# Row blocks of 113 and 15 rows per partition instead of 112 and 16 in a streaming ReLU row sum

## The chip, the cores and the metric

One core of a Trainium2 chip runs the kernel. The metric is the device time of one execution in microseconds (us), median over several runs.

## The reference

```python
def setup_inputs():
    return {"x": np.random.randn(32, 512, 1024).astype(np.float32)}

def reference(x):
    relu_x = np.maximum(x, 0)
    return np.sum(relu_x, axis=-1).astype(np.float32)
```

67.11 MB come in, 16,384 sums of 4 bytes go out.

## The kernel before

The 16,384 rows are two blocks. In the first, partition p holds 112 rows that follow each other in memory, in the second 16. So the input is read at a pitch of 448 KiB and 64 KiB from partition to partition, and the results of one partition are 448 and 64 bytes that follow each other in the output.

```python
REGIONS = [112, 16]
CHUNKS = [(0, 0), (0, 16), ..., (0, 96)]     # 7 loads of 16 rows per partition
TAIL = [8, 4, 2, 1]                          # then pieces of the second block
LAST = [512, 512]                            # and its last row in two halves

    xv = [xr[P * s : P * (s + n), :].rearrange("(p j) d -> p j d", p=P) for s, n in zip(start, REGIONS)]
    ov = [of[P * s : P * (s + n)].rearrange("(p j) -> p j", p=P) for s, n in zip(start, REGIONS)]
    # ... all loads are issued by SyncE into three buffers, then:
    sp.wait_ge(s_fact, 1)                    # last rows of chunk 6 are summed
    sp.wait_ge(s_fdve, 1)
    for g in range(len(REGIONS) - 1):        # the first store: 128 pieces of 448 bytes
        sp.dma_start(out=ov[g][:, :], in_=res[:, start[g] : start[g] + REGIONS[g]]).then_inc(s_store, 16)
    # ... ScalarE and VectorE share the rows; at the end ScalarE sums the first half of the
    # last row, VectorE adds the second half to it:
    on_act(buf[:, tb, BIG - 1, 0 : LAST[0]], last[:, LAST[1] : LAST[1] + 1]).then_inc(s_tact, 1)
    dve.wait_ge(s_tact, 1)
    dve.wait_ge(s_in[-1], 16)
    on_dve(last[:, :], res[:, J - 1 : J]).then_inc(s_tdve, 1)
    sp.wait_ge(s_tdve, 1)                    # the last store: 128 pieces of 64 bytes
    sp.dma_start(out=ov[-1][:, :], in_=res[:, start[-1] : J]).then_inc(s_out, 16)
    sp.wait_ge(s_store, 16 * (len(REGIONS) - 1))
    sp.wait_ge(s_out, 16)
```

## Time and profile before

| | before |
|---|---|
| time, median of the first 3 runs | 161.53 us |
| span of the profiled run | 159.9 us |
| one chunk of 8 MiB after the other | 19.35 us |
| last store, issue to landing | 1.4 us |

The prediction below shows the main lines. In the list of DMA issues a line has the size and the time from the issue to the landing, that is until the store has been confirmed:

```profile
out_dram<-res SPq DMA_DIRECT2D x1, 56.0 KB, 10.6
out_dram<-res SPq DMA_DIRECT2D x1, 8.0 KB, 1.4
```

The first store takes 10.6 us: it is issued at 147.20, but its packets run from 156.70 to 157.28, at the end of those of the loads, the last of which is over at 157.10. The second one takes 1.4 us with nothing else in flight. All 1.4 us of it lie on the path, as the last of SyncE's own waits shows (total, number, longest, in us):

```profile
SPq L165 <- DMA out_dram<-res: 1.1, 1, 1.1
```

The wait of 1.1 us at the end is the last store, after its issue of 0.34 us. The time can so be read as four terms that add up: the time until ScalarE can start on the first chunk (21.82), the stretch of loads until it starts on the first half of the last row (to 156.95), the sums and hand-overs until the last store is issued (to 158.45), and the store until the end (to 159.9).

### The profile page before, as it was taken

Reading aid. Unit: us, or ns where it says so; the run is one execution under the profiler, and the core shown is the slowest. Engines: PE = TensorE matmul, PEld = TensorE weight load, DVE = VectorE, ACT = ScalarE, POOL = GpSimd, SP = SyncE. Lnnn points to the kernel's source line nnn. Section 1 sums busy time; section 2 is a strip of 40 time slices with the busy share of each in tenths; the row PEclk is TensorE's granted clock in tenths of the full one; section 3 lists DMA queues with packets and bytes.
Section 4 is the critical chain, followed back from the end, with each engine's and each line's share of the span. In section 5 each row is a group of like instructions: output and inputs, shape, how many; then the busy total and the mean of one; then the engine's idle time right before and its main releaser. Section 6 shows DMA issues by size and latency. Waiting matters only on the chain.

```text
span 159.9 us, 145 instructions
## 1 busy us (share of the span) xinstructions
DVE 122.0 (76%) x56; ACT 101.0 (63%) x55; POOL 0.2 (0%) x4
## 2 busy tenths in 40 slices
DVE  0000006989889897998969989699899999598995
ACT  3000059990799708996099941999339980596972
POOL 0000000000000000000000000000000000000000
DMA  7996996996996997997989979969969969899993
GB/s 262 525 525 262 525 525 262 525 525 262 525 508 279 525 459 328 525 443 344 525 361 426 525 311 475 525 262 525 525 262 525 525 262 525 385 402 393 420 409 105
DMA packets 2160, 67.18 MB, mean 420 GB/s; under 512 B 496, under 2 KB 496, under 8 KB 880
## 3 DMA queue, kind: packets, MB, share of 16 engines
q1 hardware_dynamic: 2160, 67.18, 97.9%
HBM read 67.11 MB, written 0.07 MB: 420 GB/s over the span
## 4 chain that ended last, share of the span: by engine, by line
DMA 69%; ACT 18%; DVE 10%; SPq 1%; issue 0%
DMA buf<-in_x_dram 69%; ACT buf L128 18%; DVE res L130 10%; SPq L88 1%; ACT buf L108 0%; DVE last L111 0%
## 5 line engine op out<-in xcount | busy, mean ns | idle before, releaser
L130 DVE TENSOR_REDUCE res<-buf 128x4 f32<-128x4096 f32 (+3 forms) x18 | 100.4, 5604 | 33.5 <-ACT buf L128 33.5
L128 ACT ACTIVATE buf<-buf 128x4096 f32<-128x4096 f32 (+3 forms) x18 | 80.8, 4553 | 46.3 <-DMA buf<-in_x_dram 46.3
L108 ACT ACTIVATE buf<-buf 128x1024 f32<-128x1024 f32 (+1 forms) x18 | 18.4, 1021 | 9.7 <-DMA buf<-in_x_dram 9.7
L111 DVE TENSOR_SCALAR_CACHE_REDUCE buf<-buf 128x1024 f32<-128x1024 f32 x18 | 21.0, 1216 | 2.7 <-DMA buf<-in_x_dram 2.5
L108 ACT ACTIVATION_READ_ACCUMULATOR buf<-buf 128x1 f32 x18 | 3.4, 187 | 0.0
L128 ACT ACT_TABLE_LOAD x1 | 1.3, 1283 | 0.8 <-PEq L179 0.8
L111 DVE DVE_READ_ACCUMULATOR buf<-buf 128x1 f32 x18 | 1.5, 82 | 0.0
L111 DVE TENSOR_SCALAR_CACHE_REDUCE last<-last 128x513 f32<-128x513 f32 x1 | 0.7, 690 | 0.2 <-ACT buf L108 0.2
L179 POOL MEMSET const-uint8-127<- 128x1 uint8 x1 | 0.1, 103 | 0.0
L179 POOL MEMSET const-bfloat16-1.0<- 128x1 bf16 x1 | 0.1, 102 | 0.0
L179 POOL MEMSET const-float32-0.0<- 128x1 f32 x1 | 0.1, 99 | 0.2 <-issue 0.2
L179 POOL MEMSET const-float32-1.0<- 128x1 f32 x1 | 0.1, 99 | 0.0
L111 DVE DVE_READ_ACCUMULATOR last<-last 128x1 f32 x1 | 0.1, 82 | 0.0
## 6 DMA issues: line engine op xcount, KB each, us to landing
buf<-in_x_dram SPq DMA_DIRECT2D x1, 4096.0 KB, 26.7
buf<-in_x_dram SPq DMA_DIRECT2D x1, 2048.0 KB, 31.2
buf<-in_x_dram SPq DMA_DIRECT2D x1, 1024.0 KB, 33.2
buf<-in_x_dram SPq DMA_DIRECT2D x1, 512.0 KB, 34.0
buf<-in_x_dram SPq DMA_DIRECT2D x1, 256.0 KB, 34.2
last<-in_x_dram SPq DMA_DIRECT2D x1, 256.0 KB, 34.4
buf<-in_x_dram SPq DMA_DIRECT2D x7, 36.3
out_dram<-res SPq DMA_DIRECT2D x1, 56.0 KB, 10.6
```

What stands on the lines that cost most here:

```text
L88: sp.dma_start(out=buf[:, tb, r : r + n, :], in_=xv[-1][:, r : r + n, :]).then_inc(s_in[NBIG + i], 16)
L108: return act.activation(t, t, AF.Relu, accum_out=acc)
L111: return dve.tensor_scalar(out=t, in0=t, scalar1=0.0, scalar2=None, op0=ALU.max, op1=ALU.add, accum_out=acc)
L128: act.activation(t, t, AF.Relu).then_inc(s_act, 1)
L130: dve.tensor_reduce(out=res[:, c * BIG + r : c * BIG + r + n], in_=t, axis=X, op=ALU.add).then_inc(s_dve, 1)
L179: nc = _bacc.Bacc("TRN2", target_bir_lowering=False, num_devices=1)
```

## The change

The row blocks become 113 and 15 rows. Row 112 of the first block is loaded as the last whole piece of the tail. So both pitches of the input change (452 and 60 KiB), the last store has 15 columns instead of 16, and the first one, now of 113 columns, can only go out when row 112 is summed. The intent is a smaller store at the very end, and pitches that are no multiples of 64 KiB; that either saves time no run here had shown.

```diff
-REGIONS = [112, 16]
+REGIONS = [113, 15]
-TAIL = [8, 4, 2, 1]
+TAIL = [(1, 0, 8), (1, 8, 4), (1, 12, 2), (0, 112, 1)]     # region, first row, rows
@@ loads of the tail
-    for i, n in enumerate(TAIL):
-        sp.dma_start(out=buf[:, tb, r : r + n, :], in_=xv[-1][:, r : r + n, :]).then_inc(
+    for i, (g, j, n) in enumerate(TAIL):
+        sp.dma_start(out=buf[:, tb, r : r + n, :], in_=xv[g][:, j : j + n, :]).then_inc(
@@ the first store
     sp.wait_ge(s_fact, 1)
     sp.wait_ge(s_fdve, 1)
+    sp.wait_ge(s_rdve, 1)
@@ sums of the tail
-        for i in range(r, r + n):
-            f = on_act if (i - r) % 2 else on_dve
-            f(buf[:, tb, i, :], res[:, j0 + i : j0 + i + 1])
+        for i in range(n):
+            f = on_act if i % 2 else on_dve
+            ins = f(buf[:, tb, r + i, :], res[:, j + i : j + i + 1])
+    ins.then_inc(s_rdve, 1)
```

More of the change, by code (lines that the diff above doesn't have):

```diff
@@ L36, in bass_relu_sum_kernel @@
     NBIG = len(CHUNKS)
-    assert BIG * NBIG + sum(TAIL) + 1 == J == sum(REGIONS) and sum(LAST) == D
+    assert BIG * NBIG + sum(n for _, _, n in TAIL) + 1 == J == sum(REGIONS) and sum(LAST) == D
     xr = x.rearrange("b s d -> (b s) d")
@@ L57, in bass_relu_sum_kernel @@
     s_fdve = nc.alloc_semaphore("s_fdve")
+    s_rdve = nc.alloc_semaphore("s_rdve")
     s_tact = nc.alloc_semaphore("s_tact")
@@ L86, in bass_relu_sum_kernel @@
     tail = []
-    for i, n in enumerate(TAIL):
-        sp.dma_start(out=buf[:, tb, r : r + n, :], in_=xv[-1][:, r : r + n, :]).then_inc(
+    for i, (g, j, n) in enumerate(TAIL):
+        sp.dma_start(out=buf[:, tb, r : r + n, :], in_=xv[g][:, j : j + n, :]).then_inc(
             s_in[NBIG + i], 16
         )
-        tail.append((r, n, s_in[NBIG + i]))
+        tail.append((r, n, s_in[NBIG + i], start[g] + j))
         r += n
-    sp.dma_start(out=buf[:, tb, r, 0 : LAST[0]], in_=xv[-1][:, BIG - 1, 0 : LAST[0]]).then_inc(
+    sp.dma_start(out=buf[:, tb, r, 0 : LAST[0]], in_=xv[-1][:, REGIONS[-1] - 1, 0 : LAST[0]]).then_inc(
         s_in[-2], 16
     )
-    sp.dma_start(out=last[:, 0 : LAST[1]], in_=xv[-1][:, BIG - 1, LAST[0] : D]).then_inc(
+    sp.dma_start(out=last[:, 0 : LAST[1]], in_=xv[-1][:, REGIONS[-1] - 1, LAST[0] : D]).then_inc(
         s_in[-1], 16
@@ L136, in bass_relu_sum_kernel @@
                 on_act(*row(c, i))
-    j0 = NBIG * BIG
     for c in range(NTWO, NBIG):
@@ L146, in bass_relu_sum_kernel @@
                 ins.then_inc(s_fact if i % 2 else s_fdve, 1)
-    for r, n, s in tail:
+    for r, n, s, j in tail:
         if n > 1:
```

## The prediction

> **What bounds the kernel now.** I read four views in this order: the summary page, the chain of work that ended last in order of time, the timeline of the engines, and the DMA view of the last five microseconds. The page first:
>
> ```profile
> span 159.9 us, 145 instructions
> DMA packets 2160, 67.18 MB, mean 420 GB/s; under 512 B 496, under 2 KB 496, under 8 KB 880
> DMA 69%; ACT 18%; DVE 10%; SPq 1%; issue 0%
> ```
>
> The input of 67.11 MB has to come in once. The mean of 420 GB/s is over the whole span, head and tail included. The rate in the steady part comes from the timeline, from the starts of ScalarE's work on two successive 8 MiB chunks:
>
> ```profile
> 21.82 14.04 ACT L128 ACTIVATE buf<-buf 128x4096 f32<-128x4096 f32 x3 [19.75 <-DMA buf<-in_x_dram]
> ...
> 41.13 14.04 ACT L128 ACTIVATE buf<-buf 128x4096 f32<-128x4096 f32 x3 [5.27 <-DMA buf<-in_x_dram]
> ...
> 60.48 3.62 ACT L128 ACTIVATE buf<-buf 128x4096 f32<-128x4096 f32 x1 [5.32 <-DMA buf<-in_x_dram]
> ...
> 99.19 14.04 ACT L128 ACTIVATE buf<-buf 128x4096 f32<-128x4096 f32 x3 [5.30 <-DMA buf<-in_x_dram]
> ```
>
> Each chunk lands 19.35 us after the one before it (60.48 - 41.13, and twice that from 60.48 to 99.19), whatever the compute engines do, and ScalarE waits over 5 us for each. 8,388,608 bytes in 19.35 us is 433.5 GB/s. So the loads are the bound from the first byte on, and the compute parts that the chain shows lie beside loads. What remains beyond the loads is the end:
>
> ```profile
> 122.75 34.18 DMA buf<-in_x_dram
> 156.93 0.02 issue
> 156.95 0.73 ACT buf L108 x2
> 157.68 0.05 issue
> 157.73 0.69 DVE last L111 x2
> ```
>
> After the first half of the last row has landed at 156.93, ScalarE sums it (0.73 us), VectorE sums the other half with that result (0.69 us), and the last store goes out. The timeline of the same stretch shows VectorE's last whole row and the two stores:
>
> ```profile
> 147.20 0.35 SPq L102 DMA_DIRECT2D out_dram<-res  x1
> ...
> 156.28 1.22 DVE L111 TENSOR_SCALAR_CACHE_REDUCE buf<-buf 128x1024 f32<-128x1024 f32 x1
> ...
> 157.43 0.08 DVE L111 DVE_READ_ACCUMULATOR buf<-buf 128x1 f32 x1
> ...
> 158.45 0.34 SPq L163 DMA_DIRECT2D out_dram<-res  x1
> ```
>
> The DMA view from 155 to 160 us, 40 slices of 0.125 us, shows when the DMA engines are busy:
>
> ```profile
> DMA  9997999999999998320000000000000000330000
> ```
>
> Loads and the first store fill it up to slice 17 (157.2 us). Then there is nothing for about 2 us, and the two digits in slices 34 and 35 (159.25 to 159.5) are the last store. The first store, though issued at 147.20, landed 10.6 us later, at 157.8; the last one took 1.4 us.
>
> [...] the first store's 448-byte packets start at 156.70, 9.5 us after the issue[...].
>
> **The change part by part.**
>
> 1. The amount and order of loading. Seven chunks of 16 rows, then pieces of 8, 4, 2, 1 rows and two halves, as before: 67.11 MB, the same number of transfers of the same sizes from the same engine. Order of instructions and waits on VectorE and ScalarE is the same line by line; only the first store has one wait more. Change: 0.
>
> 2. The addresses. Row blocks start every 452 KiB instead of 448, and in the second region every 60 KiB instead of 64. Rows stay multiples of 4 KiB. Could the tail gain from the new pitch? The packet records give the mean time of one packet on its engine, by size: 65,536 B 2418 ns (median), 32,768 B 1213, 16,384 B 615, 8,192 B 312, 4,096 B 159, 2,048 B 86. From the first two, 32,768 B cost 1205 ns, which is 27.2 GB/s for one engine and 435 for 16; what is left over is 8 to 11 ns a packet at every size. From 137.90 (the last chunk has landed) to 156.93, 15.5 rows of 524,288 B come in, 8.126 MB, which at 433.5 GB/s is 18.75 us; it took 19.03. The difference of 0.28 us is what the extra packets cost: per engine 5 x 8 = 40 packets instead of 7.75 for the same bytes in 64 KiB packets, some 32 x 9 ns = 0.29. Nothing is left over for the pitch of 64 KiB to explain. Change: 0.
>
> 3. The first store moves. Before it waited for the last rows of chunk 6 (147.0); now for row 112, which is the last whole row of the tail. VectorE is done with it at 157.43 + 0.08 = 157.51. From VectorE's end to the issue of the last store before is 158.45 - 158.42 = 0.03 us, so the first store is issued at about 157.54 and SyncE is free again at 157.89, 0.56 us before it has to issue the last store. The last store's first packet came at 159.29, 0.84 us after its issue; so the first store's packets start near 158.38. Each engine has 8 of them at 25 ns, 0.2 us, and the engines are spread over some 0.2 us, as the last store's were (159.29 to 159.50): they end near 158.8. The last store's packets begin at 159.29, on empty queues again. With the 0.35 us from last packet to landing that the last store shows, the first store lands near 159.15, 0.7 us before the last. Estimates all, from these rows. On the path: 0. Loads are not helped either: the first store stood behind them.
>
> 4. The last store writes 128 x 60 bytes instead of 128 x 64. Packets of 64 B take 8 to 11 ns; 4 bytes less is worth nothing. Pieces of 60 bytes no longer start on multiples of 64, so neighbouring partitions write into the same 64 bytes. I allow 0.05 us for this.
>
> 5. A semaphore increment at row 112's sum on VectorE: it is attached to an instruction that is there anyway. VectorE was done at 157.51 and waited for ScalarE until 157.68, so even 0.1 us would be hidden.
>
> Sum: +0.05 us on a span of 159.9; the time is 1.63 us over the span before (161.53), so 161.58, which I round to 161.6.
>
> **The rivals.** First: the pitch matters, and the tail gets faster.[...] Against it: the packet times of point 2. At most the 0.28 us would be won: 161.3. Second: the new pitch does harm. Transfers of 64 KiB no longer start on 64 KiB; if each were cut once more, 56 more packets per engine at 8 ns would cost 0.45 us: 162.0.[...] Third: the two stores collide, and the last waits behind the first, or the first lands last. The margin is about 0.5 us by point 3; if the first store were to begin 0.5 us later than I think, the last would be put off by the 0.2 us of its packets, or its landing would set the end: up to 0.3 us, 161.8. Fourth: the unaligned 60-byte writes land in 1.8 instead of 1.4 us: 162.0.
>
> **Range and chances.** All but one of these lie between 161.3 and 162.0. Times of before lie within 0.05 us on one chip; another chip or day may move by some 0.1 us more. I give 161.3 to 162.1 for 8 in 10. Faster by 2% would need 3.2 us, and no more than 0.3 is there to be had: 0.01. Slower by 2% needs a loading rate 2% lower, which only the new pitch could bring: 0.02. Within 2%: 0.97.
>
> **What would show it right or wrong.** Right: chunks still land 19.35 us apart; the first half of the last row lands within 0.1 us of 156.93; the last five microseconds of the DMA view show a second island of digits near 158.4 to 158.8 that was joined to the loads before; the first store's time to landing falls from 10.6 to about 1.6 us; the last store's stays at 1.4 to 1.5. Wrong: chunks further apart than 19.5 us or nearer than 19.3 (the pitch matters after all), a last store that takes over 1.7 us, or a wait of SyncE at the end that is put down to the first store.

## The result, and the profile after

The changed kernel takes 161.99 us (median of 6 runs, 161.94 to 162.39), the kernel before 161.56 (6 runs, 161.49 to 161.76). The ratio is 1.0029, with a 95% interval of 1.0016 to 1.0042. A ratio here is the mean time of one kernel's fast runs over that of the other's of the same rounds, so it is not quite the ratio of the medians. The change costs 0.3%, far within 2%, but it is clear of the noise.

The profiled run was the longest of the six (162.39). Its page:

```profile
span 160.7 us, 145 instructions
DMA packets 2160, 67.18 MB, mean 418 GB/s; under 512 B 496, under 2 KB 496, under 8 KB 880
```

As many packets and bytes as before. The timeline has the start of the chunks:

```profile
22.20 14.04 ACT L130 ACTIVATE buf<-buf 128x4096 f32<-128x4096 f32 x3 [20.14 <-DMA buf<-in_x_dram]
...
41.52 14.04 ACT L130 ACTIVATE buf<-buf 128x4096 f32<-128x4096 f32 x3 [5.27 <-DMA buf<-in_x_dram]
...
60.88 3.62 ACT L130 ACTIVATE buf<-buf 128x4096 f32<-128x4096 f32 x1 [5.32 <-DMA buf<-in_x_dram]
```

The first chunk is there 0.38 us later than before (22.20 against 21.82). From then on a chunk takes 19.36 us (60.88 - 41.52), as it did. The end of the chain of waits:

```profile
123.18 34.14 DMA buf<-in_x_dram
157.31 0.02 issue
157.34 0.73 ACT buf L110 x2
158.07 0.02 issue
158.09 0.70 DVE last L113 x2
```

157.34 - 22.20 is 135.14 us; before it was 156.95 - 21.82 = 135.13. The whole stretch of loads, tail with its new pitch included, is unchanged to 0.01 us. The two stores in SyncE's timeline:

```profile
158.00 0.35 SPq L104 DMA_DIRECT2D out_dram<-res  x1
158.82 0.34 SPq L165 DMA_DIRECT2D out_dram<-res  x1
```

The last one is issued 1.48 us after ScalarE's start at 157.34 (before: 1.50). The DMA engines from 155 to 160 us, in slices of 0.125 us as in the prediction:

```profile
DMA  8999999999999962100000000000001870000430
```

The predicted second island is there: the first store's packets, in slices 30 to 32 (158.75 to 159.125; by the packet records they end at 159.19). They are done before the last store's packets begin (slices 37 and 38). The list of issues and SyncE's wait at the end:

```profile
out_dram<-res SPq DMA_DIRECT2D x1, 56.5 KB, 2.0
out_dram<-res SPq DMA_DIRECT2D x1, 7.5 KB, 1.8
```

```profile
SPq L167 <- DMA out_dram<-res: 1.5, 1, 1.5
```

The last store takes 1.8 instead of 1.4 us, although it moves less. The span has grown by 0.8 us, of which 0.38 came before the first chunk and 0.43 (160.71 - 158.82 = 1.89, before 159.91 - 158.45 = 1.46) after the last store's issue. This run is 0.4 us longer than the changed kernel's median, so not all of the 0.8 us is the change. That was the question for the experiments.

### The profile page after: what moved, and what is told of

Its sections match the earlier page's. It is cut to its first block, busy times and chain, and to the rows that moved or that the text cites. A ratio compares the mean times of both kernels' runs of the same rounds, so it can differ in the third digit from the quotient of the medians.

```text
span 160.7 us, 145 instructions
## 1 busy us (share of the span) xinstructions
DVE 122.0 (76%) x56; ACT 101.0 (63%) x55; POOL 0.2 (0%) x4
## 2 busy tenths in 40 slices
DMA packets 2160, 67.18 MB, mean 418 GB/s; under 512 B 496, under 2 KB 496, under 8 KB 880
## 3 DMA queue, kind: packets, MB, share of 16 engines
q1 hardware_dynamic: 2160, 67.18, 97.4%
## 4 chain that ended last, share of the span: by engine, by line
DMA 69%; ACT 18%; DVE 10%; SPq 1%; issue 0%
DMA buf<-in_x_dram 69%; ACT buf L130 17%; DVE res L132 9%; SPq L89 1%; ACT buf L110 0%; DVE last L113 0%
```

## The experiments

They went out in three calls, each on one chip, each run with five rounds against the kernel before on the same chip. The numbers are in this table, which is worked out from the profiles: start of ScalarE on the first chunk; from there to its start on the last row's first half; from there to the issue of the last store; from there to the end of the span. Row pitch is that of the loads in rows, pieces are those of the first and the last store in bytes.

| run | pitch | pieces | first chunk | loads | sums | last store | ratio (95% interval) |
|---|---|---|---|---|---|---|---|
| before | 112 | 448, 64 | 21.82 | 135.13 | 1.50 | 1.46 | |
| changed | 113 | 452, 60 | 22.20 | 135.14 | 1.48 | 1.89 | 1.0029 (1.0016 to 1.0042) |
| e1_late_store | 112 | 448 late, 64 | 21.89 | 135.14 | 1.48 | 1.50 | 1.0002 (0.9989 to 1.0014) |
| e2_store_shape | 112 | 452, 60 | 21.95 | 135.14 | 1.50 | 2.09 | 1.0038 (1.0024 to 1.0052) |
| e3_load_pitch | 113 | 448, 64 | 22.01 | 135.12 | 1.51 | 1.46 | 1.0009 (0.9996 to 1.0021) |
| e4_row112_first | 113 | 452, 60 | 21.99 | 135.20 | 1.60 | 1.82 | 1.0047 (1.0034 to 1.0059) |
| f1_source_shift | 112 | 448, 64 | 21.76 | 135.15 | 1.52 | 1.45 | 1.0004 (0.9991 to 1.0016) |
| f2_own_line | 112 | 448, 60 of 64 | 21.95 | 135.14 | 1.51 | 1.59 | 1.0006 (0.9992 to 1.0020) |
| f3_pieces_32 | 120 | 480, 32 | 21.96 | 135.18 | 1.48 | 1.46 | 1.0016 (1.0003 to 1.0028) |
| f4_pieces_16 | 124 | 496, 16 | 22.06 | 135.21 | 1.47 | 1.47 | 1.0029 (1.0016 to 1.0042) |
| g_last_60 | 112 | 448, 60 | 21.83 | 135.13 | 1.50 | 1.47 | 1.0005 (0.9994 to 1.0017) |
| g_last_48 | 112 | 448, 48 | 21.94 | 135.12 | 1.48 | 1.67 | 1.0016 (1.0004 to 1.0028) |
| g_last_4 | 112 | 448, 4 | 21.75 | 135.13 | 1.50 | 6.98 | 1.0340 (1.0311 to 1.0370) |
| g_last_64_shift | 112 | 448, 64 shifted | 21.88 | 135.15 | 1.49 | 1.47 | 0.9991 (0.9978 to 1.0004) |

A profile is one run, while the ratio is of five or six, so the terms of a row and its ratio need not agree to 0.1 us. The first call ran on chip 2, the second on chip 14, the third on chip 11. In the diffs below, new semaphores and lines that only repeat a change are cut.

### First call: pitch, lateness, or the shape of the stores

The theory (W) was that stores in unaligned pieces take longer to be confirmed. Rivals were that two stores close together hurt (S), and that the new pitch of the loads costs at the start (P).

**e1_late_store** moves the first store alone:

```diff
     sp.wait_ge(s_fdve, 1)
+    sp.wait_ge(s_rdve, 1)
@@ after the loop over the tail
-            f(buf[:, tb, i, :], res[:, j0 + i : j0 + i + 1])
+            ins = f(buf[:, tb, i, :], res[:, j0 + i : j0 + i + 1])
+    ins.then_inc(s_rdve, 1)
```

> The kernel before with one thing moved: its first store (112 columns, aligned) waits for the last whole row of the tail, as in the changed kernel. Theory W (the 60- and 452-byte pieces, which are not aligned to 64 bytes, take about 0.4 us longer to be confirmed): 161.6 us, the last store lands 1.4 us after its issue. Rival S (two stores 0.8 us apart get in each other's way, or the last store's completion waits for the writes of the first): 162.0 us, the last store lands after about 1.8 us. Rival P (the new pitch of the loads costs 0.4 us): 161.6 us.

Measured: 161.53 us against 161.47. The result is right. The list of issues of this run:

```profile
out_dram<-res SPq DMA_DIRECT2D x1, 56.0 KB, 1.6
out_dram<-res SPq DMA_DIRECT2D x1, 8.0 KB, 1.5
```

The stores are as close together as in the changed kernel (issued at 157.69 and 158.51), and it costs nothing that the timing shows (1.0002, interval 0.9989 to 1.0014). S falls as a matter of lateness alone. There is a second reading: the same late first store takes 1.6 us in pieces of 448 bytes and 2.0 us in pieces of 452.

**e2_store_shape** keeps the loads of before and stores 113 and 15 columns, the first store early:

```diff
-    ov = [... for s, n in zip(start, REGIONS)]
+    OUTS = [113, 15]
+    ostart = [0, 113]
+    ov = [... for s, n in zip(ostart, OUTS)]
@@ and res[:, ostart...] in both stores; the first waits for the first row of the tail
```

> The loads of before (pitch of 112 and 16 rows), but the results are stored as 113 and 15 columns, 452 and 60 bytes a piece, the first store early (its wait is met by the first row of the tail, near 149 us). The result is wrong on purpose (rows end up at other places of the output). Theory W: 162.0 us, the last store lands about 1.8 us after its issue. Rival S: 161.6 us and 1.4 us. Rival P: 161.6 us.

Measured: 162.12 us against 161.47; the result is wrong. The list of issues:

```profile
out_dram<-res SPq DMA_DIRECT2D x1, 56.5 KB, 8.9
out_dram<-res SPq DMA_DIRECT2D x1, 7.5 KB, 2.0
```

The first store was issued at 149.07 and had landed at 158.0, before the last was issued at 158.59. Nothing of the loads has changed, and the last store takes 2.0 us. The shape of the stores is enough to cost what the change costs, as W expects.

**e3_load_pitch** is the other half: the loads of the changed kernel, the stores of before.

```diff
+    OUTS = [112, 16]
+    ostart = [0, 112]
-    ov = [... for s, n in zip(start, REGIONS)]
+    ov = [... for s, n in zip(ostart, OUTS)]
-    sp.wait_ge(s_rdve, 1)
```

> The loads of the changed kernel (pitch of 113 and 15 rows), but the results are stored as 112 and 16 columns, early and aligned, as before. The result is wrong on purpose. Theory W: 161.6 us, the last store lands after 1.4 us. Rival S: 161.6 us. Rival P: 162.0 us, with the first chunk landing some 0.4 us later than the 21.8 us of before, as it did in the profile of the changed kernel (22.2).

Measured: 161.61 us against 161.47, wrong. The last store takes 1.4 us again:

```profile
out_dram<-res SPq DMA_DIRECT2D x1, 8.0 KB, 1.4
```

The first chunk is there at 22.01, and the ratio of 1.0009 has an interval that includes 1. So P is not the main part. It may be a small one, though: in the table, the first chunk comes at 21.75 to 21.95 in all nine profiles with a pitch of 112 rows (mean 21.86), and at 21.96 to 22.20 in all five with another pitch (mean 22.04). The gap of 0.18 us is about what e3 shows in its ratio (0.0009 x 161.5 = 0.15 us). It is suggested by the profiles, and not settled by the timing: the latest of the nine and the earliest of the five lie only 0.01 us apart, and the runs were not all on one chip.

**e4_row112_first** leaves the changed kernel as it is but loads row 112 first, so that its first store goes out early:

```diff
-TAIL = [(1, 0, 8), (1, 8, 4), (1, 12, 2), (0, 112, 1)]
+TAIL = [(0, 112, 1), (1, 0, 7), (1, 7, 4), (1, 11, 2), (1, 13, 1)]
-    ins.then_inc(s_rdve, 1)
+            if r == 0:
+                ins.then_inc(s_rdve, 1)
```

> The changed kernel with row 112 loaded first of the tail (pieces of 1, 7, 4, 2, 1 rows and two halves), so that its first store goes out some 10 us earlier, behind the loads as before; the last store keeps its 60-byte pieces. One transfer more, worth under 0.1 us. The result is right. Theory W: 162.0 us, the last store lands after 1.8 us. Rival S: 161.6 us and 1.4 us. Rival P: 162.0 us and 1.4 us.

Measured: 162.29 us against 161.47, right. The list of issues, and the end of the chain of waits:

```profile
out_dram<-res SPq DMA_DIRECT2D x1, 56.5 KB, 9.6
out_dram<-res SPq DMA_DIRECT2D x1, 7.5 KB, 1.8
```

```profile
157.98 0.02 DVEq L161
158.00 0.07 issue
158.07 0.69 DVE last L113 x2
```

Taking the first store out of the end does not bring the 1.8 us back to 1.4. W holds here too. Its ratio is 0.3 us above the changed kernel's; the profile shows 0.06 us of that in the loads (one transfer more) and 0.12 in the sums. VectorE's last piece of work starts 0.07 us after ScalarE's sum, because the second half of the last row was confirmed at 157.95: three of its 16 confirmations came 0.25 us after the other 13. The first store's packets run at that time (156.76 to 157.54; before the change 156.70 to 157.28).

### Second call: what about those pieces

**f1_source_shift** moves the last 16 results one column on in SBUF, so that the last store reads from the same address in the row as the changed kernel's, and writes as before:

```diff
-    res = nc.alloc_sbuf_tensor("res", [P, J], fp32)
+    res = nc.alloc_sbuf_tensor("res", [P, J + 1], fp32)
-    sp.dma_start(out=ov[-1][:, :], in_=res[:, start[-1] : J]).then_inc(s_out, 16)
+    sp.dma_start(out=ov[-1][:, :], in_=res[:, start[-1] + 1 : J + 1]).then_inc(s_out, 16)
```

> The kernel before, its output pieces unchanged (64 bytes, aligned to 64), but the last 16 results lie one column further on in SBUF, so that the last store reads from an address that is 452 bytes into the row, as in the changed kernel. The result is right. Theory D (what costs 0.4 us is where the pieces lie in the output): same as before, the last store lands 1.4 us after its issue. Rival R (it is the unaligned address that is read): 1.8 us, and 0.4 us more of time.

Measured: 161.53 us against 161.56, right, with 1.4 us to landing. The address that is read made no difference here. R falls.

**f2_own_line** writes 60 bytes, but each piece within its own 64:

```diff
-    sp.dma_start(out=ov[-1][:, :], in_=res[:, start[-1] : J]).then_inc(s_out, 16)
+    sp.dma_start(out=ov[-1][:, 1:], in_=res[:, start[-1] + 1 : J]).then_inc(s_out, 16)
```

> The kernel before, but the last store leaves out the first of its 16 columns: 60 bytes a piece, each within 64 bytes of its own, since the pieces still start every 64 bytes (at 4). The result is wrong on purpose, column 112 is not written. Theory L (two partitions that write into the same 64 bytes are what costs): 1.4 us to landing, as before. Rival F (a piece that does not fill its 64 bytes costs, shared or not): 1.8 us, 0.4 us more of time.

Measured: 161.60 us against 161.56, wrong. 1.5 us to landing. Pieces that don't fill their 64 bytes cost 0.1 us here (interval -0.1 to 0.3), less than the 0.4 us that F expects, so F falls as stated.

**f3_pieces_32** and **f4_pieces_16** are right versions of the kernel with other blocks:

```diff
-REGIONS = [113, 15]
-TAIL = [(1, 0, 8), (1, 8, 4), (1, 12, 2), (0, 112, 1)]
+REGIONS = [120, 8]                                          # f3
+TAIL = [(0, 112, 8), (1, 0, 4), (1, 4, 2), (1, 6, 1)]
+REGIONS = [124, 4]                                          # f4
+TAIL = [(0, 112, 8), (0, 120, 4), (1, 0, 2), (1, 2, 1)]
```

(Cut: in both, the first store waits for the sums of the last two rows of the first block, one on VectorE and one on ScalarE.)

> Row blocks of 120 and 8 rows: pieces of 480 bytes, and at the end of 32 bytes, which start on multiples of 32; two partitions share each 64 bytes. The first store waits for row 119, near 152 us, and lies behind the loads. The result is right. If pieces have to be whole units of 64 bytes: about 1.8 us to landing and 0.4 us over before. If units of 32 bytes are enough: 1.4 us and no difference.

> Row blocks of 124 and 4 rows: pieces of 496 bytes, and at the end of 16 bytes, four partitions to each 64 bytes, two to each 32. The first store waits for row 123, near 155 us. The result is right. With units of 64 or of 32 bytes: 1.8 us or more to landing, 0.4 us or more over before, more than the pieces of 32 bytes if the number of partitions that share a unit counts. If it were only that pieces straddle a boundary, these would not: 1.4 us and no difference.

Measured: 161.74 and 161.98 us against 161.56. In both profiles the last store takes 1.4 us, as if sharing 64 bytes among two or four partitions cost nothing. But f4's profiled run was the fastest of its five (161.71; the others 161.94 to 162.22), and where the others lost 0.2 to 0.5 us more can't be read from it. The 0.2 and 0.3 us that the two profiles do show lie before the first chunk (0.14 and 0.24) and in the loads (0.05 and 0.08). These two runs are inconclusive on the store.

### Third call: the last store alone

The last store of before is replaced and nothing else. Three theories on what in its pieces costs were to be told apart: two DMA engines write into the same 64 bytes (E; which engine writes which partition no trace here shows, so what E forecasts for each run rests on an assumption), pieces straddle multiples of 64 (B), pieces start elsewhere than on multiples of 16 (M).

```diff
-    sp.dma_start(out=ov[-1][:, :], in_=res[:, start[-1] : J]).then_inc(s_out, 16)
+    n = 15                                # g_last_60; 12: g_last_48; 1: g_last_4
+    tight = of[P * start[-1] : P * (start[-1] + n)].rearrange("(p j) -> p j", p=P)
+    sp.dma_start(out=tight, in_=res[:, J - n : J]).then_inc(s_out, 16)
```

```diff
+    sp.wait_ge(s_store, 16 * (len(REGIONS) - 1))                   # g_last_64_shift
+    lower = of[P * start[-1] - 4 : P * J - 4].rearrange("(p j) -> p j", p=P)
+    sp.dma_start(out=lower, in_=res[:, start[-1] : J]).then_inc(s_out, 16)
```

> The kernel before with its first store and all its loads as they are; only the last store is another: the last 15 columns, as 60-byte pieces packed without gaps. Wrong on purpose (as the next three): not all of the output is written, or not where it belongs. If the last store's pieces are the whole cause: 1.8 us or more to landing, about 162.0 us. If the unaligned first store is part of it: less than that. Three theories on what in those pieces costs all expect this one to be slow: E (two DMA engines write into the same 64 bytes[...]), B (pieces that straddle a multiple of 64 bytes), M (pieces that do not start on a multiple of 16 bytes).

Measured: 161.69 us against 161.56, with 1.4 us to landing in the profile (a run of 161.52):

```profile
out_dram<-res SPq DMA_DIRECT2D x1, 7.5 KB, 1.4
```

This was not expected by any of the three theories. The same 60-byte pieces, packed as tightly as the changed kernel's, cost 0.1 us on average when the first store has pieces of 448 bytes, and 0.6 us in e2, where it has pieces of 452. So the last store's pieces are probably not the whole cause. Three cautions: the profile caught one of the two fastest of five runs, and the two slowest (161.86 and 161.93, spans of 160.2 and 160.3 us against 159.9) may well show a late confirmation that no profile caught. e2 ran on another chip. And in e2 the last store begins 512 bytes further on in the output (byte 57,856 instead of 57,344), which no run tested.

> As the run before, with 12 columns: 48-byte pieces. They straddle multiples of 64, but start on multiples of 16[...]. Theory B: 1.8 us to landing, about 162.0 us. Theories E and M: 1.4 us, about 161.55 us.

Measured: 161.85 us against 161.56, 1.6 us to landing. Slower than E and M allow, less than B expects.

> As the runs before, with one column: 4-byte pieces. None straddles anything, but 16 of them[...] share each 64 bytes, and three of four do not start on a multiple of 16. Theories E and M: 1.8 us or more to landing, about 162.0 us. Theory B: 1.4 us, about 161.55 us.

Measured: 166.89 us against 161.56. The list of issues and SyncE's wait at the end:

```profile
out_dram<-res SPq DMA_DIRECT2D x1, 0.5 KB, 6.9
```

```profile
SPq L166 <- DMA out_dram<-res: 6.6, 1, 6.6
```

512 bytes in 128 pieces take 6.9 us. The packets themselves are over at 159.42, one microsecond after the issue at 158.38; its 16 confirmations then come one by one between 161.46 and 165.32. Against B, which expected nothing.

> As the kernel before, all 16 columns, but the last store's 64-byte pieces begin 16 bytes earlier in the output (on top of the end of the first region, whose store is waited for before; it has long landed). Pieces straddle multiples of 64[...], all starts are multiples of 16. Theories E and B: 1.8 us to landing, about 162.0 us. Theory M: 1.4 us, about 161.55 us.

Measured: 161.53 us against 161.56, 1.4 us to landing. Pieces that straddle multiples of 64, and whose neighbours share 64 bytes, cost nothing here. Against E and B as stated.

No one of E, B and M fits all four runs. What the traces show, wherever the profile has a slower last store, is where the time lies: after the last packet. From the records of packets and confirmations (us; last data packet of the last store over, first and last of its 16 confirmations):

```
run               last packet   first confirmed   last confirmed   packet to last
before                159.50            159.69           159.86             0.37
g_last_60             159.51            159.73           159.89             0.38
g_last_64_shift       159.57            159.78           159.95             0.39
f2_own_line           159.65            159.86           160.15             0.50
g_last_48             159.59            159.79           160.16             0.57
e4_row112_first       159.84            160.05           160.57             0.73
changed               159.86            160.08           160.66             0.80
e2_store_shape        159.64            159.84           160.63             1.00
g_last_4              159.42            161.46           165.32             5.90
```

The first confirmation comes about 0.2 us after the last packet in all but the last line. It is some of the later ones that lag. The runs left out, e1, e3, f1, f3 and f4, have 0.36 to 0.41 us from packet to last. So in these profiles packed pieces of 32 and 16 bytes, two and four to each 64 bytes, have no lag, and 4-byte ones, sixteen to each 64, lag by over 5 us.

## Why the prediction was right or wrong

The range of 161.3 to 162.1 holds the measured 161.99, and "within 2%" came true. The point of 161.6 was 0.4 us too low. The range held because it was drawn around the rivals, the fourth of which reaches 162.0, and not because the sum was right. Step by step:

1. Amount and order of loading, predicted 0: right. 135.13 and 135.14 us from the first chunk to the last row's first half, and 2160 packets in both pages. One reading of the prediction's point 2 is off: by its own medians the time left over per packet is 8 to 13 ns and not 8 to 11 (615 ns for 16,384 B), which changes nothing in its sum.
2. Addresses, predicted 0: right for the steady part and for the tail, as the same 135.1 us shows in e3 too. Not seen was a start that is perhaps 0.15 to 0.2 us later with the other pitch (e3, and 22.04 against 21.86 over the profiles). The check that was named, the first half of the last row within 0.1 us of 156.93, failed (157.31), for this part of the time lies ahead of the first chunk.
3. The first store's move, predicted 0 on the path: right, by e1. The store came 0.10 us after VectorE's end instead of 0.03, the packets 0.85 us after the issue as predicted (158.85 - 158.00), and its packets ended 0.5 us before those of the last began. Its landing was mis-sized: 2.0 us instead of 1.6. e1 has the 1.6 with a late store in pieces of 448, which points to the pieces.
4. The stores' pieces, predicted 0.05 us, an allowance of mine that no measured number stood behind: this is the step that failed, by its size. In the profiles the last store took 0.43 us more in the changed kernel and 0.63 in e2, where the stores are all that differs, and the ratio of e2 is worth 0.6 us. The reason given was also too narrow: I looked at the 60-byte pieces alone, and by g_last_60 they cost 0.1 us (interval -0.1 to 0.3) when the first store is aligned.
5. The semaphore increment on VectorE, predicted 0: right. 1.48 us from ScalarE's start to the last store's issue, 1.50 before.

The margin of the range rested on times of before that "lie within 0.05 us on one chip". Those were three runs: nine on chip 2 spread from 161.35 to 161.76.

Of the rivals, the fourth came out in its numbers: 1.8 instead of 1.4 us, and 162.0. Its cause, the unaligned 60-byte writes, is not shown to be enough alone (g_last_60). The third, that the stores collide, is refuted by e1 as far as lateness goes.

What is shown: the main part of the cost is in the shape of the stores (e2 against e3), it lies after the last store's packets (0.80 and 1.00 us to the last confirmation against 0.37 before), and neither the first store's lateness (e1, ratio 1.0002) nor the address that is read (f1, 1.0004) makes it. What stays open: whether the first store's 452-byte pieces take part at all, and how they could delay the confirmation of a store that, in e2 and e4, is issued after they have been confirmed. In e2 the early 452-byte store itself shows no lag: its last confirmation comes 0.52 us after its last packet, as with 448 bytes before (0.53). In the changed kernel, where it is late, that is 0.79 us, against 0.38 in e1. So W, that unaligned pieces always take longer to be confirmed, is too simple. No run had pieces of 452 and 64 bytes together, which would show if the first store is enough alone; nor were g_last_60 and e2 run on the same chip. That the 452-byte pieces matter is only an argument by elimination.

## What to carry to other kernels

When a store ends a kernel, look at what comes after its last packet: here that was 0.37 us for the 8 KB of before and 5.90 us for the 512 bytes of g_last_4. The one pair of block sizes run here that keeps each partition's results on whole multiples of 64 bytes (112 and 16 floats) was faster than the three others (113 and 15, 120 and 8, 124 and 4) by 0.2 to 0.3%, though why the last two lost is not settled. And 128 packed results of 4 bytes took 6.9 us to land where 128 pieces of 64 bytes took 1.4. No layout run here changed the stretch of loads by more than 0.08 us (8 MiB took 19.35 us before and 19.36 after the change), so with 113 and 15 rows it was mainly the side effect on the stores that decided: 0.43 of the 0.8 us in the profile.
